# Scan of a bidirectional RWKV layer: old state added by quarters of the array, products reordered and moved to other slots

## The chip, the cores and the metric

The kernel runs on one core of a Trainium2 chip. A core has a matrix engine (TensorE, in the profile PE for its matmuls and PEld for its weight loads), a vector engine (VectorE, DVE), a scalar engine (ScalarE, ACT), a general engine (GpSimd, POOL) and a queue that issues most DMAs (SyncE, SP). They work beside each other and wait for one another by semaphores. Matmuls read SBUF and write PSUM, which has eight banks. The metric is the device time of one execution, in microseconds (us); lower is better. The kernel before takes 4187.79 us, the median of three runs (4182.42 to 4188.41).

## The reference

A trunk of two layers runs over two sequences, 256 and 1024 tokens of 1024 channels, with the same weights, all in fp32. The first layer mixes tokens with an RWKV-7 scan in both directions, the second with neighbourhood attention; each is followed by a squared-ReLU MLP. The change touches the scan alone. For each of 16 heads of 64 channels, and for both directions, the reference carries a 64 x 64 state S through the tokens:

```python
def step(S, inp):
    r_t, w_t, k_t, v_t, a_t, b_t = inp
    sa = jnp.einsum('bhvk,bhk->bhv', S, a_t)
    S = S * w_t[:, :, None, :] + sa[..., None] * b_t[:, :, None, :] + v_t[..., None] * k_t[:, :, None, :]
    return S, jnp.einsum('bhvk,bhk->bhv', S, r_t)
```

The outputs of both directions are added, normalized per head, scaled by `rw_lnx_g`, shifted by `rw_lnx_b`, and the bonus times v is added.

## The kernel before

The scan works in chunks of 64 tokens. Two heads stand on the two halves of the 128 partitions. `HALVES` gives, for the head e, its own half `es` and the other half `eo`. A product of 64 x 64 uses one quarter of the matrix array: which one is set by the half of the partitions that it reads and the half that it writes.

A job is 16 chunks of a pair of heads in both directions: four groups of four chunks. There are ten jobs (`scan_job`), and a job's chunks are 16 slots of the scan. The backward direction takes the chunks from the other end, so a slot handles chunk i forward and chunk 15 - i backward. All work of the scan is written as (time, function) pairs by `at`, with time in slots from the job's first slot; the list is sorted by time, and within `manual_schedule` this fixes the order of the instructions on TensorE, VectorE, ScalarE and GpSimd. An instruction that must wait holds up everything behind it on its engine. The times order the work; they don't set when it runs. The DMA queue SP is not ordered in this way.

`scan_step` is one slot. Two PSUM tiles hold its sums: `bx` has A (the first 128 columns) and the new state `sn` (the next 128); `by` has the output Y and U. Each is there twice, for even and odd slots.

- `s0` (0.64 slot early): products with v, into sn, Y and A. They need no state.
- `s1` (at 0): products with the state S, into Y and A. `s1c`: ScalarE copies A to `up`.
- `s2` (0.3): `Q` times `up` into U. `s2b` (0.32): the old state is added to sn by a product with the full 128 x 128 identity. `s2c`: ScalarE copies U to `u`.
- `s3` (0.58): products with `u`, into sn and Y. `s3c`: ScalarE scales sn to the next S, one instruction per direction.
- `s4`, `s5`: Y is copied, and in the second half of a job added to the other direction's.

So A, up, U, u, sn, S is a chain that goes through every slot.

Beside it runs the preparation of later slots and jobs:

- The early products (`prod`, tile `aps`, TensorE): eight products per group, masked by VectorE into `za`, stored to DRAM by SP. They start some 40 slots ahead (`T0`), one group every two slots.
- The rank-1 updates: the stored blocks are loaded as `mt` and `mraw` (`mload`, at `T1`); GpSimd copies `mraw` in transposed order to `mt` (`mtr`); from `T2` on VectorE inverts 32 x 32 blocks by 31 updates of `q` (lines 874, 878 and 880), spread over slots by `pace`. `q` goes through DRAM to `Q` and `qx`.
- The merges: per group a first merge (tile `yps`) and a second one (tile `qps`) on TensorE complete the inverse for 64 x 64; ScalarE copies both results.
- The chunk's products (`kprod`, tile `kps`, line 960): each of the two blocks of a chunk and head times [a, r, identity], 192 columns. `kcopy` (ScalarE, `ll`) and `kmask` (VectorE, `zz`) read them out. There is one buffer of two banks, so the next slot's products wait for both.

The early products, the merges and the post-processing's transposes (tile `zps`) share two PSUM banks (`pa`, tag `aps`). `scan_post` is the post-processing, twice per job for half of the chunks: mean, variance and scale on VectorE, squares on ScalarE, scale and shift on GpSimd, transposes through TensorE, and stores issued by GpSimd.

For the jobs from the fourth on, T0 is -41.5: rank-1 updates start at slot -21.7 and end near -11.0, that is from slot 10.3 of the job before the previous one to slot 5.0 of the previous one. The second post-processing starts at 18.9, that is at slot 2.9 of the next job.

Of the kernel before, what the change touches and what calls it, by code (L numbers as in the profile page):

```python
# [5 lines left out]
F32 = mybir.dt.float32  # L6
# [43 lines left out]
class Trunk:  # L50
# [699 lines left out]
    def scan(self):  # L750
# [32 lines left out]
        self.b_x, self.b_y = ([self.pw.tile([P, 512], F32, name=f"{nm}{i}") for i in range(2)] for nm in ("bx", "by"))  # L783
        self.pk2 = self.sctx.enter_context(tc.tile_pool(name="pk2", bufs=1, space=PSUM, reuse_waits="tile"))
        order = {mybir.EngineType.PE, mybir.EngineType.DVE, mybir.EngineType.Activation, mybir.EngineType.Pool}
        with tc.manual_schedule(engines=order):
# [11 lines left out]
    def scan_job(self, j):  # L798
# [13 lines left out]

        T0 = (-37.0, -37.0, -39.0)[j] if j < 3 else -41.5

# [3 lines left out]
        for n, (d, g) in enumerate(order):  # L818
# [20 lines left out]
            at(t - (2.0 if j else 4.0), load, E)  # L839
            for h, dt in enumerate((1.12, 1.14, 1.42)):  # L840
                at(t + dt, lambda h=h, f=prod: f(h), E)
            at(t + 1.7, store, E)


        T1 = T0 + 16.6

# [16 lines left out]
        for i in range(4):  # L863
            at(T1 + 1.5 + 0.1 * i, lambda i=i: mtr(i), E)
        T2 = T1 + 3.2
        T3, load, pace = T2, 0.0, (-11.0 - T2) / 15
        for jj in range(31, 0, -1):
# [47 lines left out]
        for n, (d, g) in enumerate(order):  # L915
# [24 lines left out]
            t = 2 * n - 5  # L940
            for dt, f in ((0.12, lambda f=merge1: f(0)), (0.14, lambda f=merge1: f(2)), (0.5, merge1c), (0.76, lambda f=merge2: f(0)), (0.78, lambda f=merge2: f(2)), (1.5, merge2c)):
                at(t + dt, f)
# [7 lines left out]
        for q in range(16):  # L950
# [3 lines left out]
            def kprod(c, g=g, d=d, pr=pr):  # L954
                if c == 0:
                    J["kp"] = self.pk2.tile([P, 2, 512], F32, name="kps", tag="kps")
                x = J["x", d, g]
                for e, (es, eo) in enumerate(HALVES):
                    for b, out in ((1, eo), (0, es)):
                        mm(J["kp"][out, e, 192 * c:192 * c + 192], x[es, b, 2 * pr + c], x[es, 2:5, 2 * pr + c], start=True, stop=True)  # L960

# [34 lines left out]
    def scan_step(self, at, J, st, grp, k, i, new, end):  # L996
# [16 lines left out]
        def s0():  # L1013
            A, Y, sn, U = banks()
            v = J["v"]
            for d, g, c, cc, m, ch in dirs:
                for e, (es, eo) in enumerate(HALVES):
                    if not end:
                        mm(sn[es, d], ll(d, g, c, e)[eo], v[eo, cc], d == 0, False)
            for d, g, c, cc, m, ch in dirs:  # L1020
                yd = 1 - d if second else d
                for e, (es, eo) in enumerate(HALVES):
                    mm(Y[eo, yd], zz(d, g, c, e)[eo, 64:128], v[eo, cc], d == 0, False)
                    mm(A[es, d], zz(d, g, c, e)[eo, 0:64], v[eo, cc], end and d == 0, new)

        def s1():
            A, Y, sn, U = banks()
            R["S"] = S = None if new else st["S"]
            if S is None:
                return  # L1030
            for d, g, c, cc, m, ch in dirs:
                yd = 1 - d if second else d
                for es, eo in HALVES:
                    mm(Y[eo, yd], J["x", d, g][es, 3, c], S[es, d], False, False)
                    mm(A[es, d], J["x", d, g][es, 2, c], S[es, d], False, True)

# [11 lines left out]
        def s2b():  # L1048
            A, Y, sn, U = banks()
            S = R["S"]  # L1050
            if S is None or end:
                return
            mm(sn, self.ident, S, False, False)

# [5 lines left out]
        def s3():  # L1060
            A, Y, sn, U = banks()
            for d, g, c, cc, m, ch in dirs:
                yd = 1 - d if second else d
                for e, (es, eo) in enumerate(HALVES):
                    if not end:
                        mm(sn[es, d], ll(d, g, c, e)[es], R["u"][es, d], False, True)
                    mm(Y[eo, yd], zz(d, g, c, e)[es, 64:128], R["u"][es, d], False, True)

# [30 lines left out]
    def scan_post(self, at, J, grp, left):  # L1099

        nc = self.nc
        for half in range(2):
# [56 lines left out]
            def tr(st=st, y=y):  # L1159
# [3 lines left out]
                for b in range(4):  # L1163
                    for k, src in enumerate((y(), bv)):
                        nc.tensor.matmul(ps[:, b], src[:, b // 2, b % 2 * 2:b % 2 * 2 + 2], swap, start=k == 0, stop=k == 1)  # L1165

            def p5(st=st, runs=runs):
                zt = self.yp.tile([P, 4, 2, 64], F32, name="zt", tag="ysq", bufs=1)
                nc.scalar.copy(zt, st["zps"])
                for x, (m, c0) in enumerate(runs):  # L1170
                    dst = self.scr["z_d"][m].rearrange("(e v) (c t) -> e v c t", e=2, t=64)
                    for par in range(2):
                        for e in range(2):
                            nc.gpsimd.dma_start(dst[e, :, c0 + par:c0 + 4:2], zt[64 * par:64 * par + 64, 2 * x:2 * x + 2, e])
            t0 = (12.9, 18.9 if left else 16.9)[half]
            if left == 0 and half == 1:
                when = (-2.0, -1.9, -0.1, 0.0, 0.1, 0.2, 0.3, 0.4, 0.5, 0.6, 0.65, 0.7, 0.9)
            else:
                when = (0.2, 0.7, 0.6, 0.95, 1.45, 1.75, 1.9, 2.05, 2.25, 2.5, 3.1, 4.36, 4.62)
            for dt, f in zip(when, (p0, lambda f=lnx: f(1), p1, p2, p2b, p2c, lambda f=p3: f(0), lambda f=p3: f(1), lambda f=p3: f(2), p4,  # L1180
# [715 lines left out]
def host_layout(inputs):  # L1896
# [25 lines left out]
        np.tile(i["na_q_g"][0], 2)[:, None], np.tile(i["na_k_g"][0], 2)[:, None]], 1)  # L1922
    o["lnx"] = np.stack([np.repeat(i[nm].reshape(8, 2, 64)[:, ::-1].transpose(1, 0, 2), 64, 0) for nm in ("rw_lnx_g", "rw_lnx_b")], 1).reshape(P, 1024)
    c = np.zeros((P, NCONST), np.float32)
# [35 lines left out]
```

## Time and profile before

| what | value |
| --- | --- |
| median of the runs | 4187.79 us |
| the profiled execution | 4184.53 us |
| its span, first to last instruction | 4182.7 us |
| granted TensorE clock, mean | 0.952 |
| the scan's 16-slot jobs between 943.0 and 1291.5 us | 348.5 us for five |

The profile has a page and views that answer questions about one execution: the busy time of each engine in given stretches, instructions in the order of time, groups of like instructions, waits with what ended them, and the chain of work that ended last. A row of the order of time has start and length in us, the engine, the line, the operation, the tile written and the tiles read, the shape, and a count where like rows are merged. In the profile, matmuls of the scan's steps all have line 998; they are told apart by tiles: `by<-up,qq` is s2, `bx<-S,cst` is s2b, `<-vv,` is s0, `<-u,` is s3, `<-S,x` is s1. fp32 matmuls stand as two instructions each.

### The profile page before, as it was taken

The numbers are of one execution on the slowest core, as the hardware profiler recorded it, in microseconds if no ns is written. First come the engines' busy times: TensorE is split into PE (matmuls) and PEld (weight loads), VectorE is DVE, ScalarE is ACT, GpSimd is POOL, SyncE is SP. The second block draws the span as 40 slices with busy tenths as digits, with TensorE's granted clock in tenths as the row PEclk, the third lists the DMA queues.
The fourth block names the chain that finished last, engine by engine and source line by source line (L and its number), as shares of the span: only waits on it lengthen the run. The fifth ranks groups of instructions, "written<-read, shape, count | busy, mean of one in ns | idle before, by whom it ended". The sixth has DMA issues, their size and how long they took to land.

```text
span 4182.7 us, 86363 instructions
## 1 busy us (share of the span) xinstructions
PE 3851.5 (92%) x34932; PEld 3226.1 (77%) x34932; DVE 2493.6 (60%) x4850; ACT 1520.2 (36%) x3651; POOL 1292.8 (31%) x1234
## 2 busy tenths in 40 slices
PE   7897879788888799999999999989988999999999
PEld 4664669677777687888888879867767888888888
DVE  7898973566665457555555562366665755555555
ACT  6776651344444442111211132455564311121111
POOL 5440001132323434222222241244344422222222
PEclk8997889899999899999999999999999999999999
DMA  3325555766655251111111115333334111111111
GB/s 110 89 94 203 201 189 150 208 169 161 169 159 132 81 163 46 36 41 41 36 36 41 41 49 165 96 78 69 82 92 148 61 36 36 41 41 41 36 36 61
DMA packets 385792, 393.45 MB, mean 94 GB/s; under 512 B 161872, under 2 KB 306480, under 8 KB 384112
## 3 DMA queue, kind: packets, MB, share of 16 engines
q1 hardware_dynamic: 331760, 315.42, 26.8%
q10 hardware_dynamic: 46704, 61.35, 4.3%
q0 software_dynamic: 6928, 11.15, 1.0%
q8 instruction: 274, 4.49, 0.5%
q14 instruction: 126, 1.03, 0.1%
HBM read 277.80 MB, written 121.24 MB: 95 GB/s over the span
## 4 chain that ended last, share of the span: by engine, by line
PE 65%; DVE 7%; ACT 2%; DMA 2%; issue 2%; POOL 2%; SPq 1%; ACTq 0%; DVEq 0%; POOLq 0%
PE ps L96 17%; PE ps L98 17%; PE ps L97 17%; PE bx L998 3%; PE by L998 2%; PE kps L960 2%; DVE q L880 1%; PE op L1875 1%; PE pt L1817 1%; PE zps L1165 1%; DVE tmp L878 1%; PE nst L1612 1%; DMA bs<-tab 1%; PE s L1799 1%; PE vps L512 1%
## 5 line engine op out<-in xcount | busy, mean ns | idle before, releaser
L1432 DVE TENSOR_TENSOR x<-ps,x 128x256 f32<-128x256 f32 x1488 | 813.6, 595 | 628.2 <-PE ps L98 628.1
L96 PE MATMUL ps<-ah,whi 128*128 128x512 f32 (+1 forms) x2304 | 843.4, 366 | 4.2 <-ACT whi L90 4.2
L98 PE MATMUL ps<-ah,wlo 128*128 128x512 f32 (+1 forms) x2304 | 823.9, 358 | 2.9 <-POOL wlo L91 2.9
L97 PE MATMUL ps<-al,whi 128*128 128x512 f32 (+1 forms) x2304 | 823.5, 357 | 0.0
L91 POOL TENSOR_TENSOR wlo<-raw,whi 128x1024 fp32r<-128x1024 f32 (+1 forms) x178 | 391.0, 2197 | 855.7 <-ACT whi L90 827.9
L96 PE MATMUL ps<-hh,whi 128*128 128x512 f32 (+1 forms) x1536 | 546.0, 355 | 14.8 <-DVE x L1432 14.8
L98 PE MATMUL ps<-hh,wlo 128*128 128x512 f32 (+1 forms) x1536 | 545.2, 355 | 0.0
L97 PE MATMUL ps<-hl,whi 128*128 128x512 f32 (+1 forms) x1536 | 544.4, 354 | 0.0
L96 PEld LDWEIGHTS ps<-ah,whi 128*128 128x128 f32 x2304 | 438.5, 190 | 78.5 <-issue 12.4
L98 PEld LDWEIGHTS ps<-ah,wlo 128*128 128x128 f32 x2304 | 437.9, 190 | 69.1 <-POOL wlo L91 3.7
L97 PEld LDWEIGHTS ps<-al,whi 128*128 128x128 f32 x2304 | 438.6, 190 | 60.0 <-issue 1.1
L90 ACT CAST whi<-raw 128x1024 fp32r<-128x1024 f32 (+1 forms) x206 | 200.7, 974 | 699.3 <-PE ps L97 631.4
L96 PEld LDWEIGHTS ps<-hh,whi 128*128 128x128 f32 x1536 | 290.7, 189 | 58.4 <-DVE x L1432 17.9
L1411 POOL TENSOR_TENSOR rl<-rl 128x512 f32<-128x512 f32 (+1 forms) x192 | 174.2, 907 | 500.3 <-PE ps L98 458.4
L98 PEld LDWEIGHTS ps<-hh,wlo 128*128 128x128 f32 x1536 | 290.9, 189 | 41.0
L97 PEld LDWEIGHTS ps<-hl,whi 128*128 128x128 f32 x1536 | 290.9, 189 | 40.7
L1410 ACT ACTIVATE rl<-ps 128x512 f32<-128x512 f32 (+1 forms) x192 | 100.8, 525 | 546.1 <-PE ps L98 546.1
L1413 ACT CAST hh<-rl 128x512 fp32r<-128x512 f32 (+1 forms) x192 | 105.5, 549 | 321.4 <-POOL rl L1411 321.3
L1414 DVE TENSOR_TENSOR hl<-rl,hh 128x512 fp32r<-128x512 f32 (+1 forms) x192 | 119.4, 622 | 151.6 <-ACT hh L1413 151.1
L965 DVE TENSOR_TENSOR zz<-kps,cst 128x512 f32<-128x512 f32 x160 | 110.1, 688 | 165.4 <-ACT ll L970 165.4
L960 PE MATMUL kps<-x 64*64 64x192 f32 x2560 | 171.4, 361 | 21.8 <-DVE zz L965 16.7
L1810 POOL TENSOR_TENSOR s<-s,mx 128x384 f32<-128x384 f32 (+1 forms) x154 | 116.7, 768 | 212.6 <-DVE mx L1809 148.8
(313 smaller groups left out, 7799.5 us busy)
## 6 DMA issues: line engine op xcount, KB each, us to landing
x<-x_d SPq DMA_DIRECT2D x88, 512.0 KB, 4.6
raw<-in_w_down_dram SPq DMA_DIRECT2D x64, 512.0 KB, 3.6
raw<-in_w_up_dram SPq DMA_DIRECT2D x64, 512.0 KB, 4.0
eab<-x_d SPq DMA_DIRECT2D x80, 256.0 KB, 4.6
x_d<-ar ACTq DMA_DIRECT2D x32, 512.0 KB, 3.2
x_d<-bk ACTq DMA_DIRECT2D x32, 512.0 KB, 4.3
bs<-tab SPq DMA_DIRECT2D x128, 96.0 KB, 4.0
v_d<-vt ACTq DMA_DIRECT2D x80, 128.0 KB, 3.8
```

The lines of the kernel that those rows point to most:

```text
L90: nc.scalar.copy(hi[:, cs], raw)
L91: lo_eng.tensor_tensor(out=lo[:, cs], in0=raw, in1=hi[:, cs].bitcast(F32), op=ALU.subtract)
L96: mm(ps, sh, mh, start=first, stop=False)
L97: mm(ps, sh, ml, start=False, stop=False)
L98: mm(ps, sl, mh, start=False, stop=last)
L960: mm(J["kp"][out, e, 192 * c:192 * c + 192], x[es, b, 2 * pr + c], x[es, 2:5, 2 * pr + c], start=True, stop=True)
L965: nc.vector.tensor_tensor(out=z, in0=src[:, :, :, :P], in1=self.mask[d].unsqueeze(1).unsqueeze(1).to_broadcast([P, 2, 2, P]), op=ALU.mult)
L998: mm = lambda out, a, b, start, stop: nc.tensor.matmul(out, a, b, start=start, stop=stop, skip_group_check=True)
L1411: nc.gpsimd.tensor_tensor(out=r[:, :n], in0=r[:, :n], in1=r[:, :n], op=ALU.mult)
L1414: nc.vector.tensor_tensor(out=hl[:, :n], in0=r[:, :n], in1=hh[:, :n].bitcast(F32), op=ALU.subtract)
L1432: nc.vector.tensor_tensor(out=xv, in0=ps[:, :n], in1=xv, op=ALU.add)
L1810: nc.gpsimd.tensor_tensor(out=s[:, :nk], in0=s[:, :nk], in1=mx[:, 2:3].to_broadcast([P, nk]), op=ALU.mult)
```

## The change

The change has these parts:

- `s2b`: the full identity product is replaced by two products, one per half, each in one quarter and with 128 columns.
- The output Y of a head is kept on the head's own half `es` instead of the other half. In s0 the products into Y read `eo` and write `es`; in s1 and s3 they read and write `es`. The constants `lnx` are rearranged to match, and the transposes of the post-processing use the identity for y and the swapped identity for the bonus.
- `s1`: all products into A come first, then all into Y.
- `kprod`: the block that would not be used is left out for one of the two blocks, so its products have 128 columns instead of 192. The tile `kps` is one fixed tile, cleared once.
- Other slots: the eight early products of a group are split in two halves a slot apart, with the mask 0.3 slot after the second; T0 is 39 or 41 slots ahead; T1 is T0 + 17.8, T2 is T1 + 3.0, and the rank-1 updates end near -10.2. The second merges move from 0.76 to 1.12, into the place between s1 and s2 of the next slot. The second post-processing starts at 20.9 instead of 18.9, and the transposes and their copy come at 5.4 and 5.7 after the start instead of 4.36 and 4.62 (not in the last job).

With these numbers, for the jobs from the fourth on, rank-1 updates go from slot 11.8 of the job before the previous one to slot 5.8 of the previous one.

```diff
+        self.kps = self.pk2.tile([P, 2, 512], F32, name="kps")
+        nc.vector.memset(self.kps, 0.0)
...
-        T0 = (-37.0, -37.0, -39.0)[j] if j < 3 else -41.5
+        T0 = (-39.0, -39.0, -41.0)[j] if j < 3 else -41.0
...
-            for h, dt in enumerate((1.12, 1.14, 1.42)):
+            for h, dt in enumerate((1.74, 2.74, 3.05)):
                 at(t + dt, lambda h=h, f=prod: f(h), E)
-            at(t + 1.7, store, E)
+            at(t + 3.3, store, E)
-        T1 = T0 + 16.6
+        T1 = T0 + 17.8
...
-        T2 = T1 + 3.2
-        T3, load, pace = T2, 0.0, (-11.0 - T2) / 15
+        T2 = T1 + 3.0
+        T3, load, pace = T2, 0.0, (-10.2 - T2) / 15
...
-            for dt, f in ((0.12, lambda f=merge1: f(0)), (0.14, lambda f=merge1: f(2)), (0.5, merge1c), (0.76, lambda f=merge2: f(0)), (0.78, lambda f=merge2: f(2)), (1.5, merge2c)):
+            for dt, f in ((0.12, lambda f=merge1: f(0)), (0.14, lambda f=merge1: f(2)), (0.5, merge1c), (1.12, lambda f=merge2: f(0)), (1.14, lambda f=merge2: f(2)), (1.5, merge2c)):
...
                 if c == 0:
-                    J["kp"] = self.pk2.tile([P, 2, 512], F32, name="kps", tag="kps")
+                    J["kp"] = self.kps
...
                     for b, out in ((1, eo), (0, es)):
-                        mm(J["kp"][out, e, 192 * c:192 * c + 192], x[es, b, 2 * pr + c], x[es, 2:5, 2 * pr + c], start=True, stop=True)
+                        w = 128 if b == 0 else 192
+                        mm(J["kp"][out, e, 192 * c + 192 - w:192 * c + 192], x[es, b, 2 * pr + c], x[es, 5 - w // 64:5, 2 * pr + c], start=True, stop=True)
...
-                    mm(Y[eo, yd], zz(d, g, c, e)[eo, 64:128], v[eo, cc], d == 0, False)
+                    mm(Y[es, yd], zz(d, g, c, e)[eo, 64:128], v[eo, cc], d == 0, False)
...
-            for d, g, c, cc, m, ch in dirs:
-                yd = 1 - d if second else d
-                for es, eo in HALVES:
-                    mm(Y[eo, yd], J["x", d, g][es, 3, c], S[es, d], False, False)
-                    mm(A[es, d], J["x", d, g][es, 2, c], S[es, d], False, True)
+            for x in (2, 3):
+                for d, g, c, cc, m, ch in dirs:
+                    yd = 1 - d if second else d
+                    for es, eo in HALVES:
+                        mm(A[es, d] if x == 2 else Y[es, yd], J["x", d, g][es, x, c], S[es, d], False, x == 2)
...
-            mm(sn, self.ident, S, False, False)
+            for es, eo in HALVES:
+                mm(sn[es], self.ident[es, es], S[es], False, False)
...
-                    mm(Y[eo, yd], zz(d, g, c, e)[es, 64:128], R["u"][es, d], False, True)
+                    mm(Y[es, yd], zz(d, g, c, e)[es, 64:128], R["u"][es, d], False, True)
...
-                        nc.tensor.matmul(ps[:, b], src[:, b // 2, b % 2 * 2:b % 2 * 2 + 2], swap, start=k == 0, stop=k == 1)
+                        nc.tensor.matmul(ps[:, b], src[:, b // 2, b % 2 * 2:b % 2 * 2 + 2], (self.ident, swap)[k], start=k == 0, stop=k == 1)
...
-            t0 = (12.9, 18.9 if left else 16.9)[half]
+            t0 = (12.9, 20.9 if left else 16.9)[half]
...
-                when = (0.2, 0.7, 0.6, 0.95, 1.45, 1.75, 1.9, 2.05, 2.25, 2.5, 3.1, 4.36, 4.62)
+                when = (0.2, 0.7, 0.6, 0.95, 1.45, 1.75, 1.9, 2.05, 2.25, 2.5, 3.1, *((5.4, 5.7) if left else (4.36, 4.62)))
...
-    o["lnx"] = np.stack([np.repeat(i[nm].reshape(8, 2, 64)[:, ::-1].transpose(1, 0, 2), 64, 0) for nm in ("rw_lnx_g", "rw_lnx_b")], 1).reshape(P, 1024)
+    o["lnx"] = np.stack([np.repeat(i[nm].reshape(8, 2, 64)[:, ::o].transpose(1, 0, 2), 64, 0) for nm, o in (("rw_lnx_g", 1), ("rw_lnx_b", -1))], 1).reshape(P, 1024)
```

## The prediction

> **What bounds the kernel now.** I read the page first, then the busy time by stretches over the scan, then the order of time of single slots on TensorE and ScalarE, then VectorE's groups inside one stretch. The page:
>
> ```profile
> span 4182.7 us, 86363 instructions
> PE 3851.5 (92%) x34932; PEld 3226.1 (77%) x34932; DVE 2493.6 (60%) x4850; ACT 1520.2 (36%) x3651; POOL 1292.8 (31%) x1234
> ```
>
> TensorE is busy for 92% of the span, but the change touches the scan alone, so the scan has to be read by itself. The next rows give length and then the busy time of PE, PEld, DVE, ACT and POOL, the granted clock, the DMA share and GB/s. The first is five jobs of 16 slots; then two pairs "rank-1 updates running" and "not running"; then the end of the scan.
>
> ```profile
> 943.00:1291.50 348.50, 300.54 (x8436) 264.60 (x8432) 224.93 (x558) 149.80 (x590) 109.19 (x155) 0.92 0.65 164
> 1015.70:1060.30 44.60, 37.32 (x1111) 32.82 (x1099) 37.66 (x97) 20.25 (x80) 10.68 (x13) 0.96 0.55 155
> 1060.30:1086.20 25.90, 22.91 (x598) 20.31 (x602) 7.43 (x16) 9.62 (x38) 11.19 (x19) 0.87 0.76 177
> 1086.20:1130.20 44.00, 39.10 (x1108) 34.49 (x1099) 37.55 (x97) 20.39 (x80) 10.67 (x13) 0.88 0.58 162
> 1130.20:1152.20 22.00, 19.91 (x594) 17.70 (x598) 7.45 (x16) 9.69 (x38) 11.21 (x19) 1.00 0.82 176
> 1337.40:1429.00 91.60, 81.47 (x2414) 70.98 (x2411) 35.76 (x67) 49.94 (x191) 34.55 (x43) 0.98 0.36 101
> ```
>
> A job takes 348.5 / 5 = 69.7 us. A stretch with rank-1 updates (10.7 slots) takes 44.3 on average, and VectorE works 37.6 of it; the other 5.3 slots take 24.0 with 7.4 of VectorE. So VectorE nearly bounds two thirds of a job, and TensorE's chain the rest. What a slot costs where VectorE is idle, from the starts of ScalarE's copy of u, and the post-processing's transposes in the chain that ended last:
>
> ```profile
> 1088.34 0.27 ACT L1058 COPY u<-by 128x128 f32<-128x128 f32 x1 [0.43 <-PE by L998]
> 1092.24 0.27 ACT L1058 COPY u<-by 128x128 f32<-128x128 f32 x1 [0.43 <-PE by L998]
> 1095.37 0.27 ACT L1058 COPY u<-by 128x128 f32<-128x128 f32 x1 [0.44 <-PE by L998]
> 1113.24 1.98 PE zps L1165 x16
> ```
>
> Slots alternate between 3.90 (an early product and a second merge) and 3.13 (a first merge): 3.51 on average. One short slot on TensorE and ScalarE in order of time (start, length):
>
> ```profile
> 1014.18 0.45 PE L998 MATMUL by<-up,qq 64*64 64x64 f32 x8 [0.44 <-ACT up L1040]
> 1014.56 0.49 PE L998 MATMUL bx<-S,cst 128*128 128x128 f32 x2
> 1014.97 0.28 PE L998 MATMUL bx<-vv,ll 64*64 64x64 f32 x2
> ...
> 1015.14 0.22 PE L998 MATMUL bx<-vv,ll 64*64 64x64 f32 x1
> ...
> 1015.20 0.23 PE L998 MATMUL bx<-vv,ll 64*64 64x64 f32 x2
> ...
> 1015.39 0.27 PE L998 MATMUL bx<-u,ll 64*64 64x64 f32 x2
> 1015.43 0.23 PE L998 MATMUL bx<-vv,zz 64*64 64x64 f32 x2
> ...
> 1015.61 0.22 PE L998 MATMUL bx<-u,ll 64*64 64x64 f32 x1
> ...
> 1015.66 0.33 PE L960 MATMUL kps<-x 64*64 64x192 f32 x1
> ...
> 1016.32 0.28 PE L998 MATMUL bx<-S,x 64*64 64x64 f32 x2
> ...
> 1016.64 0.22 PE L998 MATMUL bx<-S,x 64*64 64x64 f32 x1
> 1016.69 0.61 PE L923 MATMUL yps<-qx,za 64*64 64x32 f32 x16
> 1017.30 0.45 PE L998 MATMUL by<-up,qq 64*64 64x64 f32 x8
> ```
>
> ```profile
> 1014.73 0.27 ACT L1058 COPY u<-by 128x128 f32<-128x128 f32 x1 [0.43 <-PE by L998]
> 1015.94 0.52 ACT L1073 ACTIVATE S<-bx,dall 128x64 f32<-128x64 f32 x2 [0.78 <-PE bx L998]
> 1016.98 0.27 ACT L1040 COPY up<-bx 128x128 f32<-128x128 f32 x1
> ```
>
> I call the four 64x64 parts of the array quarters: "straight" where input and output partitions are the same half, "crossed" where not. Every fp32 product is two instructions. In one quarter, instructions of 64 columns start 0.058 apart (1015.14 to 1015.20; yps: 8 per quarter, (0.61 - 0.22) / 7 = 0.056); those of 192 columns 0.165 apart (kps: four per quarter from 1015.66 to 1016.32). For 128 columns I take the middle, 0.110. u is copied by 1015.00, but its first product starts at 1015.39: the full-array product of the old state and the products with v stand before it.
>
> **The change part by part**, each time from a slot's first U product (by<-up,qq).
>
> *Old state in quarters.* Today the straight quarters are free at about 0.28 (1014.46), and the next 64x64 product starts at 0.79: 0.51 for two instructions. After: two instructions of 128 columns per straight quarter, 0.22, from 0.28 to 0.50.
>
> *Output rows of the other half.* The products with v (24 instructions) become all crossed: 12 per quarter, 0.70 instead of the eight, 0.46, of today. Those with u become all straight: 8 per quarter, 0.46 instead of 0.23. What decides is whether crossed work runs beside straight work queued ahead of it:
>
> ```profile
> 1019.73 0.41 PE L832 MATMUL aps<-eab 64*64 64x64 f32 x8
> 1019.92 0.37 PE L960 MATMUL kps<-x 64*64 64x192 f32 x1
> 1019.96 0.28 PE L832 MATMUL aps<-eab 64*64 64x64 f32 x3
> ```
>
> Here crossed kps products start while straight aps products, earlier in the program, still start. So the products with v can start between 0.2 and 0.4 and end between 0.9 and 1.1; I take 0.9, since this row is of the same kind. u ends at 0.82 and its products start 0.05 later (up ends 1017.25, U starts 1017.30): 0.9 in place of 1.21.
>
> *S, A, U.* The last product into the state is then the sixth of its quarter: 0.9 + 0.05 + 0.29 + 0.22 = 1.46. S follows 0.11 later (1015.83 to 1015.94) and ends at 1.57 + 0.52 = 2.09, today at 2.28. Meanwhile kps: the crossed quarters keep four of 192 (0.66, to about 1.86), the straight have four of 128 (0.44, to 1.80), then half an early product (0.23, to 2.03). A's last product starts near 2.2 and ends at 2.45; up follows at 2.57 (0.12 as today), ends at 2.84, U could start at 2.89. Behind A stand Y with S (0.23) and one merge (0.46), today partly ahead of A or in the idle 0.44: they fill the wait and end at 2.97. Slot: 3.0, now in both parities.
>
> *Early product in two halves, its mask 0.3 slot after the second.* The count is the same. Its bank is held 1.3 slots; the merges use the other of the two banks in turn, freed by ScalarE over half a slot before, so no wait: nothing. The loads keep their slots within the group and SP's store waits for the mask as now, so SP stands one more group behind its loads: nothing. Per job, rank-1 updates start 1.5 slots later and take 10.0 slots instead of 10.7.
>
> *Second post-processing two slots later.* It leaves most of the rank-1 stretch. VectorE's groups in 1015.7 to 1060.3, two post-processings each:
>
> ```profile
> L965 DVE TENSOR_TENSOR zz<-kps,cst 128x512 f32<-128x512 f32 x11 | 7.5, 686 | 4.8 <-ACT ll L970 4.8
> L1132 DVE TENSOR_TENSOR y<-y,mu 128x512 f32<-128x512 f32 x2 | 1.4, 688 | 0.0
> L1140 DVE TENSOR_REDUCE va<-ysq 128x8 f32<-128x512 f32 x2 | 1.4, 678 | 0.0
> L1157 DVE TENSOR_TENSOR y<-y,rqr 128x512 f32<-128x512 f32 x1 | 0.7, 684 | 0.0
> ```
>
> Three large operations move out, 0.69 + 0.68 + 0.68 = 2.05, and 0.7 slot of zz, 0.48: 37.6 - 2.5 = 35.1. ScalarE's square, logarithm and exponential go along, into slots where it is idle too; GpSimd's two operations and eight z_d issues also, from ahead of the rank-1 updates' copies (slot 7.5) to behind them (10.6). VectorE does not work 6.7 today (44.3 - 37.6), 4.8 of that waiting for ll. A faster TensorE shortens this wait; bounds are 2 (small pauses alone) and 6.7 (no shorter). I take 4.7: the slots without post-processing are TensorE's today, but will be VectorE's. Stretch: 35.1 + 4.7 = 39.8, down 4.5.
>
> *Outside the stretch*, 5.3 slots now cost 5.3 x 3.51 + 2.0 (transposes) = 20.6, and 24.0 is measured: 3.4 of pauses. After: 6.0 x 3.0 + 2.0 + 3.4 = 23.4, down 0.6; the moved VectorE work fits its idle two thirds.
>
> *Sum.* Eight jobs with a stretch in the scan (jobs 2 to 9): 8 x 5.1 = 41. The last 22 slots with merges have no early product: their mean today is 3.28 (3.13, and 3.90 less aps, 0.46), down 0.28 each: 6. The start: a displaced product and mask, 0.66 + 0.69, either way, and one memset of kps, up to 2 x 0.69: 0 within 3. Constants, identity in place of the swap: same instructions, nothing. Total -47. The profiled execution took 4184.53, its span 4182.7; the median of the runs is 4187.79, 0.08% above. From that median: 4141.
>
> **A rule against it.** The Trainium skill, page "TensorE: Matmul & The Clock Gate", section "The mechanism" of Part 3, says matmuls are strict FIFO in start and end. The trace disagrees: the first product with u (1015.39) starts ahead of the last with v (1015.43), which stands before it in the program. By the rule 4155 would follow; it is the first rival.
>
> **The rivals.**
> *Products start in program order.* Crossed products then wait for the last old-state product (0.39): 0.44 + 0.70 = 1.14; S ends at 2.33, A at about 2.6, and Y with the merge ends the slot at 3.2. Outside: 6 x 3.2 + 5.4 = 24.6, up 0.6; stretch still -4.5; tail 22 x 0.08 = 2: 8 x 3.9 + 2 = 33 less, 4155. The two rows above speak against it.
>
> *VectorE's stretch doesn't shrink:* the freed time returns as waits, since zz, ll and kps use one bank in turn. Left are 8 x 0.6 + 6 = 11: 4177. For it: 4.8 us of zz waiting today though work was queued. Against: those waits end with kps, which comes earlier.
>
> *Slower: the rank-1 updates' data come too late.* Their first operation stands in VectorE's queue ahead of a zz; if the transposed copies aren't there, VectorE, kps and TensorE wait. From the load's issue to the end of GpSimd's copies today, and the first update:
>
> ```profile
> 1067.33 0.89 SPq L857 DMA_DIRECT2D mraw<-dd  x2
> 1070.47 4.78 POOL L1174 DMA_DIRECT2D z_d<-zt  x8 [4.67 <-ACT zt L1169]
> 1075.29 2.04 POOL L862 COPY mt<-mraw 64x256 f32<-64x256 f32 x4
> 1085.02 0.28 DVE L874 SCALAR_TENSOR_TENSOR q<-mt,q 128x31 f32<-128x31 f32 x1
> ```
>
> That is 10.0 us, with 7.7 to spare. After, the load stands 3.0 slots ahead: 9.0 us, and 2.0 if the transposes fall between. Each microsecond late is one per job; break-even at 5.9 (41 + 6 over 8), so at a chain of some 17 us (11.0 + 5.9). At 8 late: 8 x 8 - 47 = 17 more, 4205. For it: DMA share 0.76 to 0.82 just there. Against: 4.78 of today's 10.0 are the z_d issues ahead of the copies on GpSimd; after, they stand behind.
>
> **How the numbers follow.** Forecast 0.62, program order 0.10, no shrinking 0.14, slower 0.14. A measurement of this kernel tells about 0.2%, 8 us, from no change. Of "no shrinking" I put 0.06 within that; faster is 0.62 + 0.10 + 0.08 = 0.80, slower 0.14. Low end: VectorE's pauses at 2 (8 x 2.7 = 22 more) and most of the 3.4 outside gone (24 more): 4095. High end: beyond "no shrinking", up to no change: 4190.
>
> **What would show it.** Right: u's products start about 0.9 after U's first, equal slots near 3.0 outside the rank-1 stretch, stretches near 40 us with VectorE about 35 busy, no 128x128 product with S. Wrong: products with v starting only after the old state's; zz still waiting 5 us or more for ll per stretch; first rank-1 update waiting for GpSimd; more stretches at half clock.

## The result and the profile after

In 20 runs of each kernel the kernel after takes 4192.6 us (4183.6 to 4202.7) and the kernel before 4182.6 us: a ratio of 1.0025, interval 1.0017 to 1.0033. It is slower by 10 us; the prediction had 47 us less, 4141 from the median of 4187.79 that it started from, and gave "slower" 0.14. The profiled execution of the kernel after:

```profile
span 4198.5 us, 87027 instructions
PE 3843.4 (92%) x35188; PEld 3264.8 (78%) x35188; DVE 2497.5 (59%) x4851; ACT 1519.9 (36%) x3651; POOL 1294.8 (31%) x1234
```

Busy times by stretch, columns as in the prediction: the whole scan from the first copy of u to the last slot; then "rank-1 updates running" and "not running" twice. Below it the same of the kernel before.

```profile
771.30:1438.00 666.70, 553.01 (x16400) 528.89 (x16397) 415.24 (x1005) 295.06 (x1162) 208.09 (x291) 0.93 0.56 152
...
1024.40:1069.20 44.80, 37.13 (x1069) 35.97 (x1069) 36.99 (x94) 18.27 (x72) 10.48 (x14) 0.88 0.52 150
1069.20:1096.40 27.20, 22.04 (x713) 21.36 (x708) 8.29 (x19) 12.72 (x50) 11.60 (x19) 1.00 0.73 174
1096.40:1139.00 42.60, 33.66 (x980) 32.85 (x982) 36.88 (x94) 16.64 (x66) 10.52 (x14) 0.88 0.54 159
1139.00:1166.10 27.10, 23.87 (x747) 22.96 (x744) 8.39 (x19) 12.81 (x51) 11.57 (x19) 0.98 0.75 179
```

```profile
765.20:1430.70 665.50, 572.20 (x16147) 501.35 (x16140) 415.58 (x1010) 295.23 (x1162) 206.26 (x291) 0.92 0.59 152
1014.50:1059.90 45.40, 38.12 (x1138) 33.51 (x1134) 38.05 (x100) 20.65 (x82) 10.33 (x12) 0.96 0.56 156
1059.90:1085.00 25.10, 22.11 (x562) 19.61 (x562) 7.04 (x14) 9.22 (x37) 11.54 (x19) 0.86 0.77 177
```

Of the 15.8 us between these two executions (4198.5 less 4182.7), the scan holds 1.2 (666.7 less 665.5). The scan starts 6.1 later (771.3 against 765.2), and what follows it takes 8.5 longer (4198.5 less 1438.0, against 4182.7 less 1430.7). So the 47 us that the scan should have lost are missing whole: it is as long as before.

The single slot came out as forecast. ScalarE's copies of u at the ends of two slots, then TensorE from the U products before the second copy on:

```profile
1055.13 0.27 ACT L1062 COPY u<-by 128x128 f32<-128x128 f32 x1 [3.65 <-PE by L1001]
...
1058.12 0.27 ACT L1062 COPY u<-by 128x128 f32<-128x128 f32 x1 [0.50 <-PE by L1001]
1059.16 0.52 ACT L1077 ACTIVATE S<-bx,dall 128x64 f32<-128x64 f32 x2 [0.61 <-PE bx L1001]
...
1061.10 0.27 ACT L1062 COPY u<-by 128x128 f32<-128x128 f32 x1 [0.50 <-PE by L1001]
```

```profile
1057.59 0.37 PE L1001 MATMUL by<-up,qq 64*64 64x64 f32 x6
...
1057.85 0.27 PE L1001 MATMUL bx<-S,cst 64*64 64x128 f32 x1
...
1058.43 0.28 PE L1001 MATMUL bx<-u,ll 64*64 64x64 f32 x2
1058.49 0.22 PE L1001 MATMUL bx<-vv,zz 64*64 64x64 f32 x1
...
1059.39 0.44 PE L834 MATMUL aps<-eab 64*64 64x64 f32 x8
```

Slots of 2.99 and 2.98 in both parities (forecast 3.0), u's products 0.84 after U's first (forecast 0.9), the old state in products of 64x128 and none of 128x128.

What ate the gain stands in the view of waits (total us, times, longest), here of the kernel after, then of the one before:

```profile
DVE q L876 <- POOL mt L864: 49.4, 7, 8.5
...
PE kps L963 <- DVE zz L968: 30.4, 14, 4.7
...
PE zps L1169 <- DVE za L837: 14.7, 12, 2.6
```

```profile
PE kps L960 <- DVE zz L965: 13.4, 12, 3.1
DVE q L874 <- POOL mt L862: 4.7, 1, 4.7
```

Within the scan VectorE waits 49.4 us in seven places for GpSimd's copies before a first rank-1 update; kps waits for the zz queued behind it, 17 us more than before; and a wait is new, the transposes for the mask of an early product. One such wait in SP's, GpSimd's and VectorE's order of time:

```profile
1084.02 0.78 SPq L859 DMA_DIRECT2D mraw<-dd  x2
```

```profile
1089.61 1.61 POOL L864 COPY mt<-mraw 64x256 f32<-64x256 f32 x3 [12.94 <-issue]
1091.07 4.78 POOL L1178 DMA_DIRECT2D z_d<-zt  x8
1095.78 0.69 POOL L864 COPY mt<-mraw 64x256 f32<-64x256 f32 x1
```

```profile
1096.50 0.28 DVE L876 SCALAR_TENSOR_TENSOR q<-mt,q 128x31 f32<-128x31 f32 x1 [8.46 <-POOL mt L864]
```

The eight z_d issues, 4.78 us, stand between the third copy and the fourth. The second post-processing's copy and issues come at 20.9 + 5.7 = 26.6, slot 10.6 of the next job; the four copies come at T1 + 1.5 to T1 + 1.8, and T1 + 1.8 = -21.4 is slot 10.6 too. The prediction had put the issues behind all four. The load is late too: SP issues it at 1084.02 (mraw), and VectorE is free for the first update at 1088.04 (1096.50 less 8.46), 4.0 us later, where the prediction took 9.0 for its 3.0 slots.

### The profile page after: what moved, and what is told of

Its sections match the earlier page's. It is cut to its first block, busy times and chain, and to the rows that moved or that the text cites. A ratio compares the mean times of both kernels' runs of the same rounds, so it can differ in the third digit from the quotient of the medians.

```text
span 4198.5 us, 87027 instructions
## 1 busy us (share of the span) xinstructions
PE 3843.4 (92%) x35188; PEld 3264.8 (78%) x35188; DVE 2497.5 (59%) x4851; ACT 1519.9 (36%) x3651; POOL 1294.8 (31%) x1234
## 4 chain that ended last, share of the span: by engine, by line
PE 62%; DVE 8%; issue 3%; DMA 3%; POOL 3%; ACT 2%; SPq 1%; ACTq 0%; DVEq 0%; POOLq 0%
PE ps L96 17%; PE ps L98 17%; PE ps L97 17%; PE bx L1001 2%; PE by L1001 1%; DVE q L882 1%; PE kps L963 1%; DVE tmp L880 1%; PE op L1879 1%; PE pt L1821 1%; DVE zz L968 1%; POOL z_d L1178 1%; PE vps L512 1%; PE vps L513 1%; PE vps L514 1%
## 5 line engine op out<-in xcount | busy, mean ns | idle before, releaser
L963 PE MATMUL kps<-x 64*64 64x128 f32 (+1 forms) x2560 | 167.6, 327 | 43.1 <-DVE zz L968 40.2
```

Of the source, the lines that this page charges most:

```text
L963: mm(J["kp"][out, e, 192 * c + 192 - w:192 * c + 192], x[es, b, 2 * pr + c], x[es, 5 - w // 64:5, 2 * pr + c], start=True, stop=True)
```

## The experiments

Times are medians; each ratio is to runs of the kernel before beside it. The first four kernels stand beside a kernel before of 4183.6 us.

**GpSimd's issues behind the copies (zd_behind).**

```diff
-                when = (0.2, 0.7, 0.6, 0.95, 1.45, 1.75, 1.9, 2.05, 2.25, 2.5, 3.1, *((5.4, 5.7) if left else (4.36, 4.62)))
+                when = (0.2, 0.7, 0.6, 0.95, 1.45, 1.75, 1.9, 2.05, 2.25, 2.5, 3.1, *((5.4, 5.95) if left else (4.36, 4.62)))
```

> The kernel after, with one number changed: the copy of the transposes and the eight z_d issues behind it stand at 5.95 of the post-processing instead of 5.7, so that GpSimd issues them after the fourth mt copy and not before it. Theory 'late data by GpSimd's order': the first rank-1 update waits 49.4 us in seven places in the kernel after; the fourth copy now comes 4.8 us earlier in each of seven jobs, so about 7 x 4.8 = 34 us less than the kernel after, near 4159, and the wait of VectorE for mt falls to some 15 us. Rival 'the load itself is late': the copies start late whatever stands between them; the wait stays above 35 us and the time within 10 us of the kernel after, 4182 to 4193. Rival 'the bank': neither matters, TensorE's wait of zps for the mask (14.7 us) and what follows from it stay, no change.

4176.1 us, ratio 0.9989 (0.9975 to 1.0002). All four copies now end before the issues:

```profile
1074.37 2.06 POOL L864 COPY mt<-mraw 64x256 f32<-64x256 f32 x4 [12.66 <-issue]
1076.30 4.77 POOL L1178 DMA_DIRECT2D z_d<-zt  x8
```

The wait for mt's copies falls from 49.4 to 12.6 us, with 10.1 more that end with the load. The scan takes 643.2, from 769.5 to 1412.7, 23.5 less; by the medians, each against the runs of before beside it, it is 17.5 (-7.5 against +10.0). So the forecast's slower rival is at work, and the order on GpSimd's queue is more than half of its wait; it is worth half of the 34 us expected.

**Transposes on a free bank (zps_free).**

```diff
-                when = (0.2, 0.7, 0.6, 0.95, 1.45, 1.75, 1.9, 2.05, 2.25, 2.5, 3.1, *((5.4, 5.7) if left else (4.36, 4.62)))
+                when = (0.2, 0.7, 0.6, 0.95, 1.45, 1.75, 1.9, 2.05, 2.25, 2.5, 3.1, *((5.65, 5.95) if left else (4.36, 4.62)))
```

> As zd_behind, and the transposes stand at 5.65 instead of 5.4, behind the copy that frees the second merge's bank, so that they no longer take the bank that the early product holds until its mask. Theory: the wait of zps for za (14.7 us in 12 places) goes to 3 us or less, and the time falls by 5 to 15 us beyond zd_behind, near 4148. Rival: the wait only moves to the next early product or merge, the time is within 4 us of zd_behind.

4169.0 us, ratio 0.9964 (0.9951 to 0.9978): 7 below zd_behind, within the 5 to 15 expected, though the two intervals just overlap. The wait of zps for za falls from 14.7 us in the kernel after, and 17.9 in zd_behind, to 6.9 (3 or less expected). At 5.4 the second merge still holds one of the two banks until ScalarE's copy at 0.5 of that slot, so the transposes took the early product's bank and stood behind VectorE's mask. The prediction's "the merges use the other of the two banks in turn" says nothing of the transposes.

**Arithmetic and slots apart (arith_alone, slots_alone).** Each is one half of the change. arith_alone is the kernel after with the lines below turned back; slots_alone is the kernel before with just these lines (one is left out of the print: the second merges at 1.12 and 1.14 instead of 0.76 and 0.78).

```diff
-        T0 = (-37.0, -37.0, -39.0)[j] if j < 3 else -41.5
+        T0 = (-39.0, -39.0, -41.0)[j] if j < 3 else -41.0
-            for h, dt in enumerate((1.12, 1.14, 1.42)):
+            for h, dt in enumerate((1.74, 2.74, 3.05)):
-            at(t + 1.7, store, E)
+            at(t + 3.3, store, E)
-        T1 = T0 + 16.6
+        T1 = T0 + 17.8
-        T2 = T1 + 3.2
+        T2 = T1 + 3.0
-        T3, load, pace = T2, 0.0, (-11.0 - T2) / 15
+        T3, load, pace = T2, 0.0, (-10.2 - T2) / 15
...
-            t0 = (12.9, 18.9 if left else 16.9)[half]
+            t0 = (12.9, 20.9 if left else 16.9)[half]
-                when = (0.2, 0.7, 0.6, 0.95, 1.45, 1.75, 1.9, 2.05, 2.25, 2.5, 3.1, 4.36, 4.62)
+                when = (0.2, 0.7, 0.6, 0.95, 1.45, 1.75, 1.9, 2.05, 2.25, 2.5, 3.1, *((5.4, 5.7) if left else (4.36, 4.62)))
```

> The new arithmetic alone (old state in two quarters, Y on the head's own half, A's products first, 128 columns in half of the kps products, fixed kps tile), with all slots of the kernel before (early products together, second merge at 0.76, T0, T1, T2 and pace, post-processing at 18.9, transposes at 4.36 and 4.62). Theory 'the arithmetic gains, the slots lose': slots get shorter on TensorE by 0.3 to 0.5 us, the rank-1 data keep their lead of over 10 us, and the time is 15 to 30 us below the kernel before, 4153 to 4168. Rival 'VectorE bounds the stretches': slots get shorter outside them only, the time is within 8 us of the kernel before.

> The arithmetic of the kernel before with all slots of the kernel after. Theory 'the slots lose': the z_d issues stand ahead of the fourth mt copy and the load stands 3.0 slots ahead, of about 3.5 us each, so the first update is late by some 3 us per job and the transposes wait for the mask as well: 10 to 40 us above the kernel before, 4193 to 4223. Rival 'the slots gain by themselves': second merge and post-processing in idle places shorten the slots, 4170 or less.

arith_alone: 4173.5 us, ratio 0.9980 (0.9968 to 0.9992). slots_alone: 4195.8 us, ratio 1.0033 (1.0022 to 1.0044), with the same wait, VectorE for mt's copies, at 39.9 us in seven places. So the arithmetic gains 10, less than the theory's 15 to 30, and the slots lose 12 by themselves. The two halves add up to 2 more than before and the whole change to 10 more: together they cost some 8 extra, and the wait for mt's copies is longer with the new arithmetic, 49.4 against 39.9.

Four more, beside runs of before at 4181.6 us.

**More lead (lead_only, lead_zps).**

```diff
-        T0 = (-39.0, -39.0, -41.0)[j] if j < 3 else -41.0
+        T0 = (-39.0, -41.0, -43.0)[j] if j < 3 else -43.0
...
-        T2 = T1 + 3.0
+        T2 = T1 + (5.0 if j else 3.0)
```

lead_zps has the transposes at 5.65 and 5.95 besides, as in zps_free.

> The kernel after with the early products two slots earlier (T0 at 41 slots ahead for the second job, 43 from the third on), the load of mt and mraw and GpSimd's copies two slots earlier with them, and the rank-1 updates where they were (T2 = T1 + 5.0): a lead of 5 slots in place of 3, and the copies also stand ahead of the z_d issues. Transposes as in the kernel after. Theory 'late data': VectorE's wait for mt, 49.4 us in the kernel after, goes below 8 us, and the time falls by 30 to 45 us from it, to 4148 to 4162. Rival 'the bank': the wait of zps for the mask, 15 to 18 us, and what follows it hold the time within 6 us of zd_behind, 4170 to 4182.

> lead_only with the transposes and their copy at 5.65 and 5.95 as in zps_free. In zps_free the first rank-1 updates still waited 11.5 us for mt's copies and 9.8 us for its load. Theory: these 21 us go, and the time is 4168 - 21 = 4147, within 8. Rival 'VectorE bounds the stretch': the updates start earlier but VectorE works off the same queue, within 6 us of zps_free.

lead_only: 4179.2 us, ratio 0.9994 (0.9983 to 1.0005). lead_zps: 4168.8 us, ratio 0.9965 (0.9953 to 0.9978), the same as zps_free. In neither does VectorE wait for mt within the scan any more, and the time is no lower than in zd_behind (4176.1) and zps_free. In zps_free, then in lead_zps:

```profile
DVE zz L968 <- ACT ll L973: 175.0, 87, 5.8
...
DVE q L876 <- POOL mt L864: 11.5, 4, 4.7
DVE q L876 <- DMA mt<-dd: 9.8, 4, 3.4
```

```profile
DVE zz L968 <- ACT ll L973: 199.5, 97, 5.8
```

The 21.3 us of waiting for mt are gone, and VectorE waits 24.5 us longer for ll. The theory fell for what was left after zd_behind: VectorE no longer waits for data at the first update, and waits as long for ll, ScalarE's copy of kps, instead. Both times lie where the rivals had them, though not for "VectorE works off the same queue". lead_only against lead_zps shows the bank once more: 10 us.

**Rank-1 updates over 12 slots (paced12).** Against lead_zps:

```diff
-        T0 = (-39.0, -41.0, -43.0)[j] if j < 3 else -43.0
+        T0 = (-39.0, -43.0, -45.0)[j] if j < 3 else -45.0
-        T1 = T0 + 17.8
+        T1 = T0 + (19.2 if j else 17.8)
-        T2 = T1 + (5.0 if j else 3.0)
+        T2 = T1 + (3.6 if j else 3.0)
```

> lead_zps with early products another two slots ahead (43 for the second job, 45 from the third on) and the rank-1 updates spread over 12 slots instead of 10. Theory 'VectorE bounds the stretch': some 35 us of VectorE's work then meet 12 slots of 3.0 us, 36 us, so nearly every slot is TensorE's; 2 to 5 us less per job, 15 to 40 below lead_zps. Rival 'stalls by place, not by load' (post-processing and updates in the same slots): within 8 us of lead_zps.

4160.2 us, ratio 0.9940 (0.9917 to 0.9964), from four runs: 9 below lead_zps. The direction is the theory's, the size (15 to 40) is not; the interval overlaps that of lead_zps, and the rival's 8 us are not excluded.

**The old state's quarters alone (quarters_only), in the kernel before.**

```diff
-            mm(sn, self.ident, S, False, False)
+            for es, eo in HALVES:
+                mm(sn[es], self.ident[es, es], S[es], False, False)
```

> The kernel before with only the old state's product in two quarters of 128 columns. By the prediction's first step u's products start 0.29 us earlier after U's first (0.51 less 0.22); where TensorE's chain bounds, 5.3 slots in each of eight jobs and 22 slots at the end, that is (8 x 5.3 + 22) x 0.29 = 19 us: 4165. Rival: products with v hold u's products instead, or the slots with merges take the gain back, within 6 us of the kernel before.

4166.2 us, ratio 0.9964 (0.9950 to 0.9978): 15 below the kernel before, where 19 was expected. By the medians this one edit gains more than the whole arithmetic (10; the intervals just overlap). Then something else in the arithmetic loses, and two kernels look for it.

**Y on the own half, and A first (quarters_yrows, arith_no_kps).** quarters_yrows adds to quarters_only Y's products on `es`; arith_no_kps adds to that A's products ahead of Y's, the loop over x of the change.

```diff
-                    mm(Y[eo, yd], zz(d, g, c, e)[eo, 64:128], v[eo, cc], d == 0, False)
+                    mm(Y[es, yd], zz(d, g, c, e)[eo, 64:128], v[eo, cc], d == 0, False)
-                    mm(Y[eo, yd], J["x", d, g][es, 3, c], S[es, d], False, False)
+                    mm(Y[es, yd], J["x", d, g][es, 3, c], S[es, d], False, False)
-                    mm(Y[eo, yd], zz(d, g, c, e)[es, 64:128], R["u"][es, d], False, True)
+                    mm(Y[es, yd], zz(d, g, c, e)[es, 64:128], R["u"][es, d], False, True)
```

> arith_alone without the kps part (all kps products 192 columns again, tile as in the kernel before): the slots of before with the old state in quarters, Y on the head's own half and A's products first. quarters_only, which has the first of the three alone, was 15 us below the kernel before, arith_alone 10. Theory 'only the quarters count, the other parts neither help nor hurt': 15 us below the kernel before, within 5. Rival 'Y's products on the straight quarters lengthen u's products' part': 8 us or less below it. Rival 'the fixed kps tile costs': 15 or more below, and so better than arith_alone.

> quarters_only with Y's products on the head's own half; A's and Y's products with S in turn as in the kernel before (arith_no_kps without A's products first). Theory 'Y's rows cost, the order of A does not': slots of about 3.0 and 3.8, a time within 4 us of arith_no_kps, 8 below the kernel before. Rival 'A's products first cost': slots of 2.75 and 3.6, 15 below the kernel before.

arith_no_kps: 4174.5 us, beside before at 4182.3, ratio 0.9984 (0.9975 to 0.9993). It fits the rival that Y's products on the straight quarters cost (8 or less below the kernel before). quarters_yrows: 4179.1 us, beside before at 4179.1, ratio 0.9998 (0.9988 to 1.0008), 8 above what its theory gave. ScalarE's copies of u bound a long and a short slot; in quarters_only, then quarters_yrows, then arith_no_kps:

```profile
1102.41 0.27 ACT L1059 COPY u<-by 128x128 f32<-128x128 f32 x1 [2.35 <-PE by L998]
...
1105.98 0.27 ACT L1059 COPY u<-by 128x128 f32<-128x128 f32 x1 [0.43 <-PE by L998]
1106.81 0.52 ACT L1074 ACTIVATE S<-bx,dall 128x64 f32<-128x64 f32 x2 [0.40 <-PE bx L998]
...
1108.71 0.27 ACT L1059 COPY u<-by 128x128 f32<-128x128 f32 x1 [0.43 <-PE by L998]
```

```profile
1108.90 0.27 ACT L1059 COPY u<-by 128x128 f32<-128x128 f32 x1 [2.38 <-PE by L998]
...
1112.96 0.27 ACT L1059 COPY u<-by 128x128 f32<-128x128 f32 x1 [0.43 <-PE by L998]
1114.01 0.52 ACT L1074 ACTIVATE S<-bx,dall 128x64 f32<-128x64 f32 x2 [0.61 <-PE bx L998]
...
1116.09 0.27 ACT L1059 COPY u<-by 128x128 f32<-128x128 f32 x1 [0.44 <-PE by L998]
```

```profile
1105.67 0.27 ACT L1059 COPY u<-by 128x128 f32<-128x128 f32 x1 [2.60 <-PE by L998]
...
1109.50 0.27 ACT L1059 COPY u<-by 128x128 f32<-128x128 f32 x1 [0.43 <-PE by L998]
...
1112.49 0.27 ACT L1059 COPY u<-by 128x128 f32<-128x128 f32 x1 [0.50 <-PE by L998]
```

| kernel | long slot | short slot |
| --- | --- | --- |
| before | 3.90 | 3.13 |
| quarters_only | 3.57 | 2.73 |
| quarters_yrows | 4.06 | 3.13 |
| arith_no_kps | 3.83 | 2.99 |

The slots go the theory's way, and further (3.13 and 4.06 for 3.0 and 3.8). Y's rows take back all that the quarters gave, 0.40 in the short slot: S starts 1.05 after u's copy instead of 0.83, since Y's and the state's products with u then share the straight quarters, and A's products with S share them with Y's. A first wins 0.14 to 0.23 of it again; in the time that is 5 to 8 us, with intervals that overlap. A first on the old rows was not tried.

**The first job as before (paced12_start).** Against paced12; beside before at 4182.3 us.

```diff
-        T0 = (-39.0, -43.0, -45.0)[j] if j < 3 else -45.0
+        T0 = (-37.0, -43.0, -45.0)[j] if j < 3 else -45.0
-            for h, dt in enumerate((1.74, 2.74, 3.05)):
+            for h, dt in enumerate((1.74, 2.74, 3.05) if j else (1.12, 1.14, 1.42)):
-            at(t + 3.3, store, E)
+            at(t + (3.3 if j else 1.7), store, E)
-        T1 = T0 + (19.2 if j else 17.8)
+        T1 = T0 + (19.2 if j else 16.6)
-        T2 = T1 + (3.6 if j else 3.0)
+        T2 = T1 + (3.6 if j else 3.2)
-        T3, load, pace = T2, 0.0, (-10.2 - T2) / 15
+        T3, load, pace = T2, 0.0, ((-10.2 if j else -11.0) - T2) / 15
```

> paced12 with the first job's preparation in the slots of the kernel before (T0 at 37 slots ahead, early products together, T1 = T0 + 16.6, T2 = T1 + 3.2, updates ending at -11.0). In all kernels with the slots of the kernel after, the scan's first copy of u came at 769.5 to 774.0 us of the span, with the slots of before at 760.4 to 765.3. Theory 'the first job's preparation ends 0.8 slots later and holds the start': the first copy of u is back at or below 766 and the time 5 to 9 us below paced12, near 4153. Rival 'the start varies by itself': within 3 us of paced12, first u still near 770 or more.

4149.7 us, ratio 0.9924 (0.9910 to 0.9938). The time came as the theory said and its place did not: u's first copy stayed at 771.2. The theory of the start falls, and where these 11 us come from stays open; the intervals of the two kernels overlap. The scan is 615 long (771 to 1386), against 635 for paced12, in one execution each, but those executions lie 5 below and 6 above their medians. The largest pieces of the 20 us lie in jobs whose preparation the edit does not touch: by u's copies the fourth job takes 63.9 instead of 69.1, and the tenth, over its 15 steps, 54.7 instead of 60.6.

**The old rows in the new slots (paced12_y).** paced12_start with the three Y lines above turned back to `eo`, s1's loop, the transposes' operand and the order of `lnx` as in the kernel before; the quarters and kps stay. Beside before at 4179.1 us.

```diff
-            for x in (2, 3):
-                for d, g, c, cc, m, ch in dirs:
-                    yd = 1 - d if second else d
-                    for es, eo in HALVES:
-                        mm(A[es, d] if x == 2 else Y[es, yd], J["x", d, g][es, x, c], S[es, d], False, x == 2)
+            for d, g, c, cc, m, ch in dirs:
+                yd = 1 - d if second else d
+                for es, eo in HALVES:
+                    mm(Y[eo, yd], J["x", d, g][es, 3, c], S[es, d], False, False)
+                    mm(A[es, d], J["x", d, g][es, 2, c], S[es, d], False, True)
```

> paced12_start with Y on the other half and A's and Y's products with S in turn, both as in the kernel before (quarters for the old state, 128 columns in kps and all slots stay). Undisturbed slots, in us: quarters_only 2.74 and 3.57, arith_no_kps 2.99 and 3.83, so Y's rows with A's order cost 0.25 a slot there. Theory 'Y on the own half costs TensorE's straight quarters': slots of 2.75 in place of 2.99 where TensorE bounds, some 6 to 8 per job, 1.5 to 2 us per job: 12 to 18 below paced12_start, near 4135. Rival 'A behind Y takes it back, since here no early product fills the wait': slots stay at 2.95 or more, within 5 us of paced12_start.

4144.3 us, ratio 0.9917 (0.9904 to 0.9930), the lowest median of all, 35 below the kernel before and 5 below paced12_start, where 12 to 18 were expected. Three copies of u in it:

```profile
1084.27 0.27 ACT L1062 COPY u<-by 128x128 f32<-128x128 f32 x1 [0.65 <-PE by L1001]
...
1087.06 0.27 ACT L1062 COPY u<-by 128x128 f32<-128x128 f32 x1 [0.43 <-PE by L1001]
...
1089.80 0.27 ACT L1062 COPY u<-by 128x128 f32<-128x128 f32 x1 [0.43 <-PE by L1001]
```

The slot is 2.79 and 2.74 instead of 2.99, as the theory has it, but the kernel's interval overlaps that of paced12_start: the time doesn't tell the two apart. Faster slots on TensorE seem worth little by now: the scan takes 617.5 us here, not less than the 615 of paced12_start, and 3.86 on average for 160 slots.

## Why the prediction was wrong

- **Old state in quarters: right.** 0.29 a slot was forecast; the slots lost 0.33 and 0.40, and alone the edit gave 15 us of the 19 that the same 0.29 gives.
- **Output rows of the other half: its cost was counted, but never weighed by itself.** The forecast had 0.70 in place of 0.46 and 0.46 in place of 0.23 on quarters and took only the sum of all parts, a slot of 3.0. That sum was right (2.99). Split, this part takes back what the quarters give.
- **Crossed work beside straight work: right.** u's first product (1058.43) starts ahead of the last with v (1058.49) here too. The Trainium skill, page "TensorE: Matmul & The Clock Gate", section "The mechanism" of Part 3, has matmuls strict FIFO in start and end; by that rule u's products would have come later than they did. The prediction's rival of program order had them 1.14 after U's first; 0.84 was measured.
- **Second post-processing two slots later: the step that failed.** It was to take GpSimd's issues "from ahead of the rank-1 updates' copies (slot 7.5) to behind them (10.6)". That was read off the slot numbers to one decimal: at 10.6 the issues tie with the fourth copy, and they went first. zd_behind prices it: 17.5 us of medians, 23.5 in the scan. The rival "data come too late" named the wait, and the argument against it was this same sentence. The rival's 9.0 us of lead was wrong as well: in the place shown it is 4.0. Without the issues the fourth copy would have ended there near 1091.7 (an estimate: it begins at 1089.61, and four copies took 2.06 in zd_behind), still 3.7 late; in zd_behind 22.7 us of such waits are left (12.6 and 10.1). The break-even of 5.9 us per job was met about (49.4 / 8 = 6.2), and the scan came out even. That the two agree is luck in part, since mending the order gave the scan 23.5 back and not 47.
- **Early product in two halves, "so no wait: nothing": wrong** by the transposes on the same banks, 7 us (zps_free) to 10 (lead_only against lead_zps).
- **Rank-1 stretch 44.3 to 39.8: too large.** From the first update to the last a stretch took 45.4 and 44.9 us before (the prediction's rows begin 1.2 behind the first update), 44.8 and 42.6 in the kernel after, and 43.3 and 43.4 in zps_free. VectorE's work in it fell from 38.05 to 36.9, 1.1 and not 2.5. Two things were misjudged. Of the three large operations that were to move out, the `y<-y,rqr` counted once in the prediction's rows is the first post-processing's; the second's comes at 1060.95, behind the last update at 1059.64, and was never in the stretch. And three updates per stretch became long, 1.26 to 1.36 us, where one was before. One of them, one of the same shape in the next stretch, and what GpSimd does beside the first:

```profile
1066.40 1.26 DVE L882 TENSOR_TENSOR q<-q,tmp 128x87 f32<-128x87 f32 x1
...
1098.62 0.25 DVE L882 TENSOR_TENSOR q<-q,tmp 128x87 f32<-128x87 f32 x1
```

```profile
1066.29 1.26 POOL L1128 TENSOR_TENSOR bv<-bv,lnx 128x512 f32<-128x512 f32 x1 [5.17 <-DVE bv L1121]
```

All six long updates of the two stretches start 0.1 to 0.3 us behind such a product or sum of GpSimd's and end 0.1 to 0.3 behind it; the other updates take 0.22 to 0.43. With the post-processing moved, GpSimd's operations came to stand beside updates, which the forecast gave no price; they add some 3.0 us to a stretch, against 1.6 before (one update, and one `mu` of 0.75 instead of 0.17). That GpSimd is the cause rests on this coincidence; no run separates it. VectorE's pauses stayed too: 6.5 in zps_free, not 4.7, so that the rival "VectorE's stretch doesn't shrink" holds in part.
- **The end of the scan, 6 less: not seen.** From the 138th copy of u to the last it takes 76.7 us before, 78.8 in the kernel after and 82.3 in zps_free. Undisturbed slots there are 2.9 to 3.0, as forecast, but single ones take 4 to 7 (before up to 5.1); why is open.
- **The start "0 within 3": wrong by 6.** The data are late here too. The first update before the scan's first u waits 10.8 us for GpSimd's copies in the kernel after, and TensorE behind it 9.8 for a zz. It waits 9.5 to 10.0 in zd_behind, zps_free and slots_alone, 8.1 to 13.3 in the three paced12 kernels, and 1.7 to 4.3 in the five kernels with the old slots. The z_d issues have no part in it: in the kernel after GpSimd issues none in between and sits idle for 20.6 us until the load has landed. In lead_only and lead_zps that wait is gone, TensorE waits 7.7 and 7.6 for qq from DRAM instead, and u's first copy comes just as late (773.0 and 774.0); so what sets the start isn't settled.
- **After the scan: 8.5 not foreseen and not explained.** In the other kernels this part is 2754 to 2763 us, in the kernel before 2752, with no order that follows the edits.

With the two mishaps of place mended (zps_free) the change is worth 15 us, not 47. In its profiled execution the scan is 29.4 shorter than before (636.1 against 665.5; the second to the eighth job take 65.5 each instead of 69.4), but it starts 8.8 later (774.0) and what follows takes 6.1 longer. So besides the two mishaps the forecast missed 18 us by its sizes inside the scan and 15 by what it put at nothing around it.

## What to carry to other kernels

When work is moved in an order written out by hand, list for each in-order queue what stands at the new place, ties included, and for each shared buffer who holds it then; a single wrong neighbour on GpSimd took more than the arithmetic gained. Ask as well what other engines will be doing beside the new place. Price each part of an edit alone before adding them up: one part of this change, the quarters, gave 15 us without any of the rest. And a wait that goes away is a gain only if its engine has nothing else to wait for: 21 us of waiting for mt became 24 us of waiting for ll.

## What was not expected of the hardware

Which half a product writes to decides what it competes with: with the same number of instructions of the same size (quarters_only and quarters_yrows), a slot took 0.40 us longer (2.73 to 3.13) when Y's products with u and S moved from the crossed quarters to the straight ones, where the state's and A's products stand, and those with v the other way.
